# Gate operands made a block product later, in tiles of their own, ordered behind the MLP's casts one per step; the last gate tile multiplied by column halves

## The chip, the cores and the metric

The kernel runs on one core of one Trainium2 chip. The metric is device time in microseconds (us) of one launch. The kernel before took 1662.34 us, the median of three runs (1661.71 to 1663.44).

The engines in the tables: PE is the matmul engine and PEld its weight loads, DVE and ACT are the vector and the scalar engine, POOL is GpSimd, SP the engine that issues most of the DMA transfers. POOL has a DMA queue of its own.

## What is computed

One layer of an encoder with 1024 tokens and 1024 channels: a mixing part (windowed attention beside a bidirectional recurrence), then the two parts that matter here.

```python
hf = rms_norm(x, norm_ffn[i])
x = x + jnp.square(jax.nn.relu(hf @ w_ff1[i])) @ w_ff2[i]      # 1024 -> 4096 -> 1024
hp = rms_norm(x, norm_ple[i])
x = x + (p[i] @ w_ple[i]) * jax.nn.sigmoid(hp @ w_ple_gate[i])  # gate: 1024 x 1024
```

All inputs, weights and the output are float32. The change lies in the second matrix of the MLP (`w_ff2`), during which the operands of the gate matrix (`w_ple_gate`) are prepared, and in the last product of the gate.

## The kernel before, in words

**Split products.** Every float32 product is made of three matmuls on the reduced type fp32r. `split` turns a tile into a high part, a cast on ACT (line 205), and a low part, the tile minus its high part on DVE (line 206). The three terms are high x high, high x low and low x high. In names, an `h` or `l` at the end marks the parts: `sh`, `sl` of a left block and `th`, `tl` of a right block.

**Seven products instead of eight.** The matrices `w_ff2` and `w_ple_gate` are cut into 2 x 2 blocks and multiplied by the Strassen-Winograd scheme: seven block products of sums of blocks. The list `PRODS` gives their order for `w_ff2`: A11 x B11, S2 x T2, A12 x B21, S3 x T3, S1 x T1, A22 x T4, S4 x B22. In the code the loop variable `ip` counts them from 0 to 6; the text calls them product 1 to 7. Their left operands (hidden activations and their sums) lie in DRAM as `hid_...`. The right operands are blocks of `w_ff2` or sums of blocks that `right_of` makes with DVE subtractions. `t1r`, `t2r` and `b11r` are kept in the on-chip memory for a while.

**Steps.** A product has 16 steps (`p` from 0 to 15). A step loads a left block into `sst` and, where needed, a right block into `tst` (three buffers each, issued by SP, 256 KB each), splits both, and issues 12 matmuls of 512 columns on PE (line 2024): four row groups, each into its own PSUM bank, by three terms. `sh`, `sl`, `th` and `tl` have five buffers each (`NR2 = 5`) in the pool `F2`. At the end of product 1 its four banks are copied to `c1r`. At the end of every other product four additions on DVE (`add_to`, line 1881) put the banks into the result `X`. The copy `c1r` has to go into three quarters of `X` besides, in twelve more additions, which are written into the first twelve steps of product 4.

**Gate operands.** `gate_operands` is a generator that prepares the seven right operands of the gate product (T1, B11, T3, T2, B22, T4, B21) for each of four row blocks `k`. A call of it does one operand of one `k`: it makes a sum if one is needed (on DVE, line 1856, in a tile `gsum`), splits the sum or the raw block, and stores the two parts to DRAM (`gop_...`, line 1900) by POOL's queue. It also issues loads of later raw blocks (`graw`, line 1896), again by POOL's queue. The parts are put in the same tiles `th` and `tl` that the MLP's steps use. The call sites lie in products 2 to 5: one at the end of product 2, ten each in products 3 and 5, eight in product 4, and those that are left at the end of product 5 (29 calls, of which the first only loads).

```python
            if ip == 1 and p == NPR - 1 or ip in (2, 4) and p % 5 < 3 or ip == 3 and p % 2:
                next(gops, None)
```

**What sets the order.** The program is written as one sequence; a scheduler orders each engine's instructions from the dependencies and the place in the text, and hands out a tile's buffer again when its last readers are done. `after(ins, prev)` ties one instruction behind another on the same engine, in program order and without a semaphore. A matmul issued by `mmo` (line 232 in the profile) is kept in program order on PE.

**The gate product and the end.** During product 7 the first gate operands are read back from DRAM on SP (`right_gate`, line 1962) and the normed tokens are transposed. After it come the gate's seven products (`product_of`), each of four row tiles `i` of twelve matmuls. `finish` (lines 2113 to 2117) adds a bank to the collected sums, applies the tanh on ACT, multiplies by the stored `p @ w_ple`, adds to `X` and stores the output. The very last tile (A12 x B21, `i == 3`) is finished in two parts of 256 columns.

## Time and profile before

| | |
|---|---|
| median of the runs | 1662.34 us |
| profiled execution | 1661.47 us, span of its trace 1659.7 us |
| PE busy | 1599.7 us, 96% of the span, 12232 matmuls |
| PEld busy | 1291.6 us, 78% |
| DVE busy | 1175.5 us, 71% |
| ACT busy | 872.8 us, 53% |
| POOL busy | 141.3 us, 9% |
| DMA, mean over the span | 185 GB/s |

Busy times are sums over instructions and their share is of the span. Matmuls are pipelined, so their records overlap, and a PE that counts as busy need not run at its peak. Where a row says `[4.16 <-DMA gop_T<-th]`, the engine stood idle for 4.16 us just before the instruction, and the last event that released it was the DMA that stores `th` to `gop_T`. Names are cut at the first digit, so `gop_T` stands for T1, T2, T3 and T4, `gop_B` for B11, B21 and B22, and `hid_S` for S1 to S4. A group's row in the list of waits gives the total time, the number of waits and the longest.

### The profile page before, as it was taken

Reading aid. Unit: us, or ns where it says so; the run is one execution under the profiler, and the core shown is the slowest. Engines: PE = TensorE matmul, PEld = TensorE weight load, DVE = VectorE, ACT = ScalarE, POOL = GpSimd, SP = SyncE. Lnnn points to the kernel's source line nnn. Section 1 sums busy time; section 2 is a strip of 40 time slices with the busy share of each in tenths; the row PEclk is TensorE's granted clock in tenths of the full one; section 3 lists DMA queues with packets and bytes.
Section 4 is the critical chain, followed back from the end, with each engine's and each line's share of the span. In section 5 each row is a group of like instructions: output and inputs, shape, how many; then the busy total and the mean of one; then the engine's idle time right before and its main releaser. Section 6 shows DMA issues by size and latency. Waiting matters only on the chain.

```text
span 1659.7 us, 31568 instructions
## 1 busy us (share of the span) xinstructions
PE 1599.7 (96%) x12232; PEld 1291.6 (78%) x12232; DVE 1175.5 (71%) x2164; ACT 872.8 (53%) x1616; POOL 141.3 (9%) x214
## 2 busy tenths in 40 slices
PE   7999999999999999899999999999999989899998
PEld 7987777666777777677888788888888767788886
DVE  6758998378848769678637866766668767687357
ACT  5558888388554563654324544444444434455452
POOL 1440000300000000000001000000000122200201
PEclk9999999999999999999999999999999999999999
DMA  6363556954575753467721454444489866668456
GB/s 226 83 158 109 165 167 187 271 154 142 166 200 177 210 151 118 159 216 239 262 87 66 140 176 147 139 152 153 153 296 322 250 236 224 205 219 286 156 202 228
DMA packets 212167, 307.02 MB, mean 185 GB/s; under 512 B 49841, under 2 KB 106289, under 8 KB 210737
## 3 DMA queue, kind: packets, MB, share of 16 engines
q1 hardware_dynamic: 192480, 260.43, 48.8%
q0 software_dynamic: 19392, 44.05, 8.6%
q8 instruction: 96, 1.57, 0.4%
q10 hardware_dynamic: 144, 0.52, 0.1%
q14 instruction: 55, 0.44, 0.1%
HBM read 205.33 MB, written 99.61 MB: 184 GB/s over the span
## 4 chain that ended last, share of the span: by engine, by line
PE 66%; DVE 10%; DMA 9%; issue 7%; ACT 6%; POOL 2%; DVEq 0%; SPq 0%; POOLq 0%; ACTq 0%
PE ff1ps L1694 16%; PE ff2ps L2024 8%; PE gps L232 5%; PE gmm L232 4%; DMA wst<-in_w_col_dram 2%; PE mm L250 2%; PE mm L251 2%; PE mm L252 2%; PE psq L468 1%; PE psq L470 1%; PE psq L469 1%; PE mmo L252 1%; PE mmo L250 1%; PE mmo L251 1%; PE wy L232 1%
## 5 line engine op out<-in xcount | busy, mean ns | idle before, releaser
L2024 PE MATMUL ff2ps<-tl,sh 128*128 128x512 f32 x448 | 179.0, 400 | 16.9 <-DVE tl L206 16.9
L2024 PE MATMUL ff2ps<-th,sh 128*128 128x512 f32 x448 | 177.2, 396 | 1.8 <-ACT th L205 1.8
L2024 PE MATMUL ff2ps<-th,sl 128*128 128x512 f32 x448 | 176.7, 394 | 0.0
L2024 PEld LDWEIGHTS ff2ps<-tl,sh 128*128 128x128 f32 x448 | 85.5, 191 | 40.8 <-DVE tl L206 23.3
L205 ACT CAST whi<-wst 128x512 fp32r<-128x512 f32 x100 | 60.1, 618 | 86.4 <-DMA wst<-in_w_col_dram 39.8
L2024 PEld LDWEIGHTS ff2ps<-th,sh 128*128 128x128 f32 x448 | 85.5, 191 | 21.4 <-ACT th L205 3.3
L2024 PEld LDWEIGHTS ff2ps<-th,sl 128*128 128x128 f32 x448 | 85.7, 191 | 17.5
L1694 PE MATMUL ff1ps<-mh,w1h 128*128 128x512 f32 x224 | 87.5, 391 | 0.3 <-ACT w1h L205 0.3
L1694 PE MATMUL ff1ps<-ml,w1h 128*128 128x512 f32 x224 | 87.4, 390 | 0.0
L1694 PE MATMUL ff1ps<-mh,w1l 128*128 128x512 f32 x224 | 87.2, 389 | 0.0
L205 ACT CAST sh<-sst 128x512 fp32r<-128x512 f32 x109 | 67.4, 619 | 37.4 <-DMA sst<-hid_A 13.2
L206 DVE TENSOR_TENSOR sl<-sst,sh 128x512 fp32r<-128x512 f32 x109 | 74.6, 685 | 14.1 <-ACT sh L205 13.8
L205 ACT CAST w1h<-w1st 128x512 fp32r<-128x512 f32 x48 | 28.3, 619 | 98.9 <-DMA w1st<-in_w_ff_dram 64.3
L206 DVE TENSOR_TENSOR wlo<-wst,whi 128x512 fp32r<-128x512 f32 x88 | 58.9, 686 | 17.5 <-ACT whi L205 15.4
L206 DVE TENSOR_TENSOR w1l<-w1st,w1h 128x512 fp32r<-128x512 f32 x48 | 31.8, 687 | 53.4 <-ACT w1h L205 53.4
L1208 DVE TENSOR_TENSOR gm<-gps,gmask 128x384 f32<-128x384 f32 x64 | 32.7, 549 | 30.6 <-PE gps L232 30.4
L238 PE MATMUL gmm<-hh,whi 128*128 128x512 f32 x128 | 51.5, 402 | 1.8 <-ACT whi L205 1.7
L232 PE MATMUL gmm<-hh,wlo 128*128 128x512 f32 x128 | 53.2, 416 | 0.0
L206 DVE TENSOR_TENSOR w1l<-ssum,w1h 128x512 fp32r<-128x512 f32 x64 | 42.8, 685 | 14.3 <-ACT w1h L205 14.3
L232 PE MATMUL gmm<-hl,whi 128*128 128x512 f32 x128 | 52.9, 413 | 0.0
L232 PE MATMUL gmm<-hh,whi 128*128 128x512 f32 x128 | 52.8, 412 | 0.0
L242 PE MATMUL gmm<-hh,wlo 128*128 128x512 f32 x128 | 51.6, 403 | 0.7 <-POOL wlo L206 0.5
(470 smaller groups left out, 4618.9 us busy)
## 6 DMA issues: line engine op xcount, KB each, us to landing
tst<-in_w_ff_dram SPq DMA_DIRECT2D x80, 256.0 KB, 4.2
wst<-in_w_col_dram SPq DMA_DIRECT2D x76, 256.0 KB, 4.1
w1st<-in_w_ff_dram SPq DMA_DIRECT2D x32, 512.0 KB, 4.9
hid_S<-h SPq DMA_DIRECT2D x64, 256.0 KB, 2.1
sst<-hid_S SPq DMA_DIRECT2D x64, 256.0 KB, 4.0
hid_A<-h SPq DMA_DIRECT2D x48, 256.0 KB, 2.0
sst<-hid_A SPq DMA_DIRECT2D x45, 256.0 KB, 4.6
ra_d<-ra SPq DMA_DIRECT2D x8, 1024.0 KB, 5.9
```

The costliest lines, as they stand in the source:

```text
L205: a = nc.scalar.copy(hi, src)
L206: b = (lo_eng or nc.vector).tensor_tensor(out=lo, in0=src, in1=hi.bitcast(F32), op=ALU.subtract)
L232: tc.keep_in_program_order(nc.tensor.matmul(*a, **kw))
L238: mm(ps, ah, bh, start=(i == 0), stop=False)
L242: mm(ps, al, bh, start=False, stop=(i == n - 1))
L250: nc.tensor.matmul(ps, ah, bh, start=(i == 0), stop=False)
L251: nc.tensor.matmul(ps, ah, bl, start=False, stop=False)
L252: nc.tensor.matmul(ps, al, bh, start=False, stop=(i == n - 1))
L468: nc.tensor.matmul(pss[g], ah, wq[k][0][:, gs], start=(k == 0), stop=False)
L1208: a = (nc.vector.tensor_tensor(out=gm[hf][:, s % NB, e].rearrange("p (a b) t -> p a b t", b=2), in0=pss[e][:, 0:6].rearrange("p (a b) t -> ...
L1694: (mmo if p < 2 else nc.tensor.matmul)(ps, x_[:, k, :], y_[:, k, :], start=start and k + i == 0, stop=k == 3 and i == 2, skip_group_check= ...
L2024: nc.tensor.matmul(banks[bs][i], x_[:, isl], y_, start=fresh and p + j == 0, stop=p == NPR - 1 and j == 2, skip_group_check=True)
```

## The change

The diff makes five edits.

1. The parts of gate operands go into tiles `gth` and `gtl` of their own, three buffers each, in the pool `QP`. To make room, `gsum` has one buffer instead of two, T3's sum is written over the raw block B12, `QP` is opened only after product 3 in the place of `c1r`, and `QP` and `t1r` are closed after product 6 instead of product 5. Line numbers in the new program are shifted by 3 to 6 (the closing additions are line 1887, the gate operands' stores line 1906).
2. So that `c1r` is free by then, its twelve additions are written into product 3 instead of product 4.
3. The calls of the generator move: eight in product 4 (its first step and the odd ones from 3 on), fourteen in product 5 (every step from 2 on), the rest in product 6.
4. Each gate step's sum, cast and subtraction are tied by `after` behind the cast or subtraction that the MLP issued last (`paced`), on ACT and on DVE.
5. The last gate tile's twelve matmuls of 512 columns become two sets of twelve of 256 columns, the first half of the columns and then the second, in one bank.

```diff
--- before.py
+++ after.py
@@ -1824,9 +1824,13 @@
         f, n = p + NPR * (int(b[1]) - 1), int(b[2]) - 1
         return w2[f * P:(f + 1) * P, 512 * n:512 * n + 512]
 
-    def parts_of(pl, names, src_, bufs):
+    paced = []
+
+    def parts_of(pl, names, bufs, src_, behind=None):
         hi, lo = (pl.tile([P, 512], F32R, name=x_, bufs=bufs) for x_ in names)
-        split(hi, lo, src_)
+        ops = split(hi, lo, src_, behind=behind)
+        if not behind:
+            paced[:] = ops
         return hi, lo
 
     def fetch(pl, src_, name, bufs):
@@ -1836,8 +1840,8 @@
 
     pre = []
     for p in range(NPRE):
-        pre.append(parts_of(RF, ("sh", "sl"), fetch(RF, hid_d["A11"][p], "st", 1), NPRE)
-                   + parts_of(RF, ("th", "tl"), fetch(RF, w2_block(p, "B11"), "st", 1), NPRE))
+        pre.append(parts_of(RF, ("sh", "sl"), NPRE, fetch(RF, hid_d["A11"][p], "st", 1))
+                   + parts_of(RF, ("th", "tl"), NPRE, fetch(RF, w2_block(p, "B11"), "st", 1)))
     sFO.close()
     sW1.close()
     sM.close()
@@ -1851,9 +1855,11 @@
     def acc(bs, name="ff2ps"):
         return PH.tile([P, 512], F32, name=name, tag=f"acc{bs}", bufs=4)
 
-    def sum_of(op, a_, b_, out_=None):
+    def sum_of(op, a_, b_, out_=None, pace=False):
         o_ = F2.tile([P, 512], F32, name="tmp", bufs=2) if out_ is None else out_
-        nc.vector.tensor_tensor(out=o_, in0=a_, in1=b_, op=op)
+        a = nc.vector.tensor_tensor(out=o_, in0=a_, in1=b_, op=op)
+        if pace:
+            after(a, paced[1])
         return o_
 
     def t1_of(p):
@@ -1896,33 +1902,30 @@
                 nc.gpsimd.dma_start(raw[b], gate_block(k, b))
 
         def keep(k, r, src_):
-            for x_, t_ in enumerate(parts_of(F2, ("th", "tl"), src_, NR2)):
+            for x_, t_ in enumerate(parts_of(QP, ("gth", "gtl"), 3, src_, paced)):
                 nc.gpsimd.dma_start(gop_d[r][x_][:, k, :], t_.bitcast(F32))
-
-        def gsum():
-            return QP.tile([P, 512], F32, name="gsum", tag="gsum", bufs=2)
 
         raw = {}
         for b in ("B11", "B12", "B22"):
             load(0, b)
         yield
         for k in range(4):
-            t = sum_of(ALU.subtract, raw["B12"], raw["B11"], gsum())
+            t = sum_of(ALU.subtract, raw["B12"], raw["B11"], QP.tile([P, 512], F32, name="gsum", bufs=1), True)
             keep(k, "T1", t)
             yield
             keep(k, "B11", raw["B11"])
             load(k, "B21")
             yield
-            keep(k, "T3", sum_of(ALU.subtract, raw["B22"], raw["B12"], gsum()))
+            keep(k, "T3", sum_of(ALU.subtract, raw["B22"], raw["B12"], raw["B12"], True))
             load(k + 1, "B11")
             yield
-            sum_of(ALU.subtract, raw["B22"], t, t)
+            sum_of(ALU.subtract, raw["B22"], t, t, True)
             keep(k, "T2", t)
             yield
             keep(k, "B22", raw["B22"])
             load(k + 1, "B12")
             yield
-            sum_of(ALU.subtract, raw["B21"], t, t)
+            sum_of(ALU.subtract, raw["B21"], t, t, True)
             keep(k, "T4", t)
             yield
             keep(k, "B21", raw["B21"])
@@ -2016,8 +2019,8 @@
             if ip == 0 and p < NPRE:
                 sh, sl, th_, tl_ = pre[p]
             else:
-                sh, sl = parts_of(F2, ("sh", "sl"), fetch(F2, hid_d[lr_][p], "sst", 3), NR2)
-                th_, tl_ = parts_of(F2, ("th", "tl"), right_of(p, rr_), NR2)
+                sh, sl = parts_of(F2, ("sh", "sl"), NR2, fetch(F2, hid_d[lr_][p], "sst", 3))
+                th_, tl_ = parts_of(F2, ("th", "tl"), NR2, right_of(p, rr_))
             for i in range(4):
                 isl = slice(i * P, (i + 1) * P)
                 for j, (x_, y_) in enumerate(((sh, th_), (sh, tl_), (sl, th_))):
@@ -2029,10 +2032,9 @@
                 sX0.close()
                 PXX = pool(sX, "x1", side="right")
                 X = [PXX.tile([P, 4, DM], F32, name=f"X{e}") for e in range(2)]
-                c1 = pool(sC1, "c1", side="right").tile([P, 4, 512], F32, name="c1r")
                 t2r = pool(sT2, "t2", side="right").tile([P, NPR, 512], F32, name="t2r")
                 t1r = pool(sT1, "t1", side="right").tile([P, NPR, 512], F32, name="t1r")
-                QP = pool(sQP, "gprep", side="right")
+                c1 = pool(sC1, "c1", side="right").tile([P, 4, 512], F32, name="c1r")
             if ip == 0 and 0 <= p - (NPR - T1EARLY - NPRE) < NPRE:
                 q = p - (NPR - T1EARLY - NPRE)
                 nc.sync.dma_start(b11[:, q], w2_block(q, "B11"))
@@ -2042,13 +2044,10 @@
                 e, i = divmod(p // 2, 4)
                 t = torder[4 * e + i]
                 nc.sync.dma_start(X[e][:, i, :], x1_d[t * P:(t + 1) * P, :])
-            if ip == 3 and p < 12:
+            if ip == 2 and p < 12:
                 add_to(*((0, 1), (1, 1), (1, 0))[p // 4], p % 4, c1[:, p % 4])
-            if ip == 1 and p == NPR - 1 or ip in (2, 4) and p % 5 < 3 or ip == 3 and p % 2:
+            if ip == 3 and (p == 0 or p > 1 and p % 2) or ip == 4 and p > 1 or ip == 5 and p in (2, 4, 6, 8, 10, 12, 13, 14):
                 next(gops, None)
-            if ip == 4 and p == NPR - 1:
-                for _ in gops:
-                    pass
             if ip == 5 and p % 4 == 1:
                 k, nsl = p // 8, slice(512 * (p // 4 % 2), 512 * (p // 4 % 2) + 512)
                 split(wp[0][:, k, nsl], wp[1][:, k, nsl], fetch(F2, wpv[:, k, nsl], "tst", 3))
@@ -2069,17 +2068,20 @@
             else:
                 for e, n in {1: [(0, 1)], 2: [(0, 0)], 3: [(1, 1)], 4: [(1, 1)], 5: [(1, 0)], 6: [(0, 1)]}[ip]:
                     add_to(e, n, i, b_)
+        if ip == 2:
+            sC1.close()
+            QP = pool(sQP, "gprep", side="right")
         if ip == 3:
             sB11.close()
         if ip == 4:
-            sQP.close()
-            sT1.close()
             PP = pool(sP, "plew")
             wp = [PP.tile([P, 2, DM], F32R, name=f"wp{i}", bufs=1) for i in range(2)]
             pps = []
         if ip == 5:
+            assert next(gops, 0) == 0
+            sQP.close()
+            sT1.close()
             sT2.close()
-            sC1.close()
             RP = pool(sRP, "gate", side="right")
             GL["S1"], GL["A22"] = left(RP, 0), left(RP, 1)
             singles = [slice(k, k + 1) for k in range(4)]
@@ -2095,11 +2097,13 @@
     g12 = LP.tile([P, 4, 512], F32, name="g12", bufs=1)
     cs_ = {n: [LP.tile([P, 512], F32, name=n, tag=f"{n}{i}", bufs=1) for i in range(4)] for n in ("gc5", "gc4", "gc1", "gu2")}
 
-    def product_of(bank, l, r, i, fresh=True):
+    halves = (slice(0, 256), slice(256, 512), slice(0, 512))
+
+    def product_of(bank, l, r, i, fresh=True, cols=slice(0, 512)):
         (lh, ll), (rh, rl) = GL[l], GR[r]
         for k in range(4):
             for j, (x_, y_) in enumerate(((lh, rh), (lh, rl), (ll, rh))):
-                mmo(bank, x_[:, k, tsl(i)], y_[:, k, :], start=fresh and k + j == 0, stop=k == 3 and j == 2, skip_group_check=True)
+                mmo(bank[:, cols], x_[:, k, tsl(i)], y_[:, k, cols], start=fresh and k + j == 0, stop=k == 3 and j == 2, skip_group_check=True)
 
     def finish(e, n, i, name, bank, parts=1):
 
@@ -2161,7 +2165,8 @@
         finish(0, 1, i, "gu2", kept[i])
     for i in R4:
         b_ = acc(0, "gps2")
-        product_of(b_, "A12", "B21", i)
+        for c in halves[:2] if i == 3 else halves[2:]:
+            product_of(b_, "A12", "B21", i, cols=c)
         finish(0, 0, i, "gc1", b_, 2 if i == 3 else 1)
     sF.close()
     sRP.close()
```

**How instructions move.** Three places. The rows give an engine's instructions in the order of its program, with the line, the operation, output and inputs, the shape, and in brackets the semaphores waited for with their engine (`DMAHW` are transfers issued by SP, `DMASW` those issued by POOL).

On DVE, at the start of product 3: the closing additions of product 2 among the first splits of product 3. Before:

```order
L206 TENSOR_TENSOR tl<-tst,th 128x512 [waits DMAHW3_49,Activation_49]
L206 TENSOR_TENSOR tl<-graw,th 128x512 [waits DMASW1_49,Activation_49]
L206 TENSOR_TENSOR sl<-sst,sh 128x512 [waits DMAHW5_49,PE_49,Activation_49]
L1881 TENSOR_TENSOR X_13620<-X_13620,ff2ps 128x512 [waits PE_49] x4
L206 TENSOR_TENSOR tl<-tst,th 128x512 [waits DMAHW4_49,Activation_49]
L206 TENSOR_TENSOR tl<-gsum,th 128x512 [waits DMASW3_49,Activation_49]
L206 TENSOR_TENSOR tl<-tst,th 128x512 [waits DMAHW6_49,Activation_49]
L206 TENSOR_TENSOR sl<-sst,sh 128x512 [waits DMAHW7_49]
```

The change:

```order
L206 TENSOR_TENSOR tl<-tst,th 128x512 [waits DMAHW4_49,Activation_49]
L206 TENSOR_TENSOR sl<-sst,sh 128x512 [waits DMAHW5_49,PE_49,Activation_49]
L1887 TENSOR_TENSOR X_13620<-X_13620,ff2ps 128x512 [waits PE_49] x4
L1887 TENSOR_TENSOR X_13620<-X_13620,c1r 128x512 [waits DVE_49] x3
L206 TENSOR_TENSOR tl<-tst,th 128x512 [waits DMAHW6_49,Activation_49]
L1887 TENSOR_TENSOR X_13620<-X_13620,c1r 128x512 [waits DVE_49]
L206 TENSOR_TENSOR sl<-sst,sh 128x512 [waits DMAHW7_49,Activation_49]
L206 TENSOR_TENSOR tl<-tst,th 128x512 [waits DMAHW0_49,Activation_49]
```

The gate operands' subtractions (`tl<-graw`, `tl<-gsum`) have left this place, and the additions of `c1r` stand behind the closing additions. In both programs the closing additions come only after the low parts of the first three steps of the new product.

On ACT, in product 5: the casts of MLP steps and gate steps. Before:

```order
L205 CAST th<-graw 128x512 [waits DMASW3_49,DMASW2_49,DVE_49]
L205 CAST sh<-sst 128x512 [waits DMAHW7_49,PE_49]
L205 CAST th<-t1r 128x512 [waits PE_49]
L205 CAST th<-gsum 128x512 [waits DMASW5_49,DVE_49]
L205 CAST sh<-sst 128x512 [waits DMAHW2_49,PE_49]
L205 CAST th<-t1r 128x512 [waits PE_49]
L205 CAST th<-graw 128x512 [waits DMASW4_49,DMASW0_49,DVE_49]
L205 CAST sh<-sst 128x512 [waits DMAHW5_49,PE_49]
L205 CAST th<-t1r 128x512 [waits PE_49]
L205 CAST sh<-sst 128x512 [waits DMAHW6_49,PE_49]
L205 CAST th<-t1r 128x512 [waits DMASW2_49,DVE_49]
```

The change:

```order
L205 CAST gth<-gsum 128x512 [waits DMASW6_49,DVE_49,Activation_49]
L205 CAST th<-t1r 128x512 [waits PE_49]
L205 CAST gth<-graw 128x512 [waits DMASW5_49,DMASW1_49,Activation_49]
L205 CAST sh<-sst 128x512 [waits DMAHW2_49,PE_49]
L205 CAST th<-t1r 128x512 [waits PE_49]
L205 CAST gth<-gsum 128x512 [waits DMASW2_49,DVE_49,Activation_49]
L205 CAST sh<-sst 128x512 [waits DMAHW3_49,PE_49]
L205 CAST th<-t1r 128x512 [waits PE_49]
L205 CAST gth<-graw 128x512 [waits DMASW6_49,DMASW0_49,Activation_49]
```

Before, the last cast shown, of the MLP's `th`, waits for a transfer of POOL's queue; in the change the MLP's casts wait for PE alone, and the `gth` casts wait for POOL's transfers, one such cast behind each MLP step.

On DVE, at the end of the program, in the change (before it reads the same but for the line numbers):

```order
L2117 TENSOR_TENSOR gc_16962<-gc_16962,gps_17576 128x256 [waits PE_49]
L2117 TENSOR_TENSOR gc_16962<-gc_16962,gps_17576 128x256
L2119 SCALAR_TENSOR_TENSOR gc_16962<-gc_16962,pwl 128x256 [waits DMASW3_49,Activation_49]
L2119 SCALAR_TENSOR_TENSOR gc_16962<-gc_16962,pwl 128x256 [waits Activation_49]
L2120 TENSOR_TENSOR X_13620<-X_13620,gc_16962 128x256 [waits DVE_49] x2
```

The two additions of 256 columns that read the last bank stand side by side, and only the first of them carries a wait for PE.

## The prediction

> **What bounds the kernel now.** I read the product stage from coarse to fine. First the windows, cut at every 192nd matmul of line 2024, so that each row is one of the first six products of the second MLP matrix. A product is sixteen steps of twelve matmuls. Columns: length, then per engine busy time and instructions (PE, PEld, DVE, ACT, POOL), granted clock, DMA share, GB/s.
>
> ```profile
> span 1659.7 us, 31568 instructions
> ...
> 1212.34:1256.87 44.53, 44.26 (x194) 35.88 (x192) 34.90 (x55) 20.63 (x34) 0.55 (x1) 1.00 0.96 344
> 1256.87:1300.39 43.52, 43.52 (x194) 36.04 (x192) 37.76 (x61) 19.93 (x35) 1.09 (x2) 1.00 0.89 292
> 1300.39:1356.86 56.47, 48.06 (x193) 36.68 (x192) 31.93 (x52) 21.32 (x39) 12.43 (x23) 0.97 0.78 255
> 1356.86:1407.44 50.58, 46.07 (x193) 36.94 (x192) 40.19 (x67) 24.57 (x45) 10.81 (x20) 0.97 0.62 204
> 1407.44:1460.53 53.09, 47.51 (x194) 37.75 (x192) 32.80 (x54) 23.54 (x43) 12.43 (x23) 0.94 0.64 211
> 1460.53:1504.05 43.52, 43.52 (x194) 36.05 (x192) 33.75 (x55) 19.81 (x36) 0.00 (x0) 1.00 0.74 236
> ```
>
> Products 2 and 6 take 43.52 us and PE is never idle in them: the floor is 2.72 us a step. Products 3, 4 and 5 lie above it by 12.95, 7.06 and 9.57 us, 29.58 us together, and POOL, which issues the gate operands' transfers, is busy in just these three. Product 1 loses 1.01 us. No engine is full where the time is lost: DVE has 31.93 us of work in the 56.47 of product 3. So the loss is waiting, not work. The waits inside the same stretch, 1212 to 1504 (total us, times, longest):
>
> ```profile
> ACT th L205 <- DMA gop_T<-th: 25.4, 9, 4.4
> ...
> ACT th L205 <- DMA gop_B<-th: 22.9, 7, 4.7
> ...
> DVE tl L206 <- DMA gop_T<-tl: 18.2, 9, 3.6
> ...
> DVE tl L206 <- DMA gop_B<-tl: 17.3, 9, 4.5
> PE ff2ps L2024 <- DVE tl L206: 16.9, 15, 3.4
> ...
> PE ff2ps L2024 <- ACT th L205: 1.8, 3, 0.7
> ```
>
> ACT waits 48.3 us and DVE 35.5 us for the stores of gate operands, because MLP steps and gate steps draw th and tl from the same five buffers, and a buffer that held a gate operand is free only when its store has landed. PE then waits 18.7 us for tl and th. The first stall of product 3, in the timelines of ACT, POOL, DVE and PE (start, length):
>
> ```profile
> 1297.20 0.62 ACT L205 CAST th<-gsum 128x512 fp32r<-128x512 f32 x1
> ...
> 1303.64 0.62 ACT L205 CAST th<-graw 128x512 fp32r<-128x512 f32 x1 [4.16 <-DMA gop_T<-th]
> ```
>
> ```profile
> 1298.12 0.54 POOL L1900 DMA_DIRECT2D gop_T<-th  x1 [75.73 <-ACT th L205]
> ```
>
> ```profile
> 1304.29 0.69 DVE L206 TENSOR_TENSOR tl<-graw,th 128x512 fp32r<-128x512 f32 x1 [3.74 <-ACT th L205]
> 1304.90 0.69 DVE L206 TENSOR_TENSOR sl<-sst,sh 128x512 fp32r<-128x512 f32 x1
> 1305.51 2.47 DVE L1881 TENSOR_TENSOR X<-X,ff2ps 128x512 f32<-128x512 f32 x4
> 1307.90 0.69 DVE L206 TENSOR_TENSOR tl<-tst,th 128x512 fp32r<-128x512 f32 x1
> ```
>
> ```profile
> 1305.83 0.39 PE L2024 MATMUL ff2ps<-th,sh 128*128 128x512 f32 x1
> 1308.64 0.80 PE L2024 MATMUL ff2ps<-tl,sh 128*128 128x512 f32 x1 [2.42 <-DVE tl L206]
> 1309.23 0.63 PE L2024 MATMUL ff2ps<-th,sl 128*128 128x512 f32 x1
> 1309.66 0.63 PE L2024 MATMUL ff2ps<-th,sh 128*128 128x512 f32 x1
> ...
> 1312.15 0.39 PE L2024 MATMUL ff2ps<-th,sh 128*128 128x512 f32 x1
> ```
>
> One gate cast takes a buffer at 1297.20, its store is issued at 1298.12, and the next gate cast, which draws the same buffer, starts only at 1303.64, with the MLP's casts queued behind it on ACT and DVE. PE stands from 1305.83 to 1308.64. After that its matmuls start 0.43 us apart (1309.23, 1309.66), not 2.72/12 = 0.227, and the eight intervals up to 1312.15 take 3.51 us instead of 1.82: a long stall is paid again in a lower granted clock, 0.94 to 0.97 in these windows against 1.00. That is why 29.58 us are lost where the named idle time is 18.7.
>
> **The change part by part.** *Own buffers for gate operands.* gth and gtl, three each, so the MLP's five th and tl are freed by PE alone. No cast or store is added. The 83.8 us of ACT and DVE waiting on buffers that the MLP shares go. What remains is the gate operands' own set, reused after three gate steps: 8.16 us at one step per MLP step (product 5), 16.3 at one per two (products 4 and 6). What has to fit in:
>
> ```profile
> L1900 POOL DMA_DIRECT2D gop_T<-tl x16: 539/539/547, 1298.9 to 1451.5; - x16
> ...
> DMA to landing us min/median/max: 2.7/4.7/7.6
> ```
>
> The store's median 4.7 us, two POOL issues of 0.54 and a DVE subtraction of 0.69 make 6.5 us, less than 8.16. The longest, 7.6, makes 9.4, over by 1.2 us once. Queued behind such a wait stand the next MLP casts, and PE waits only when their lead is gone. On DVE the four additions that close a product, which must wait for its last matmul, stand behind the tl of the third step of the next product, so the lead there is about three steps, 8.2 us; elsewhere the five buffers allow more.
>
> *Steps moved and tied.* The 28 gate steps and their loads run in products 4 to 6 (7, 14, 7) and each stands behind the MLP casts of its step. The twelve c1 additions move into product 3 or before. DVE starts such instructions 0.60 us apart:
>
> ```profile
> 1384.04 0.68 DVE L206 TENSOR_TENSOR sl<-sst,sh 128x512 fp32r<-128x512 f32 x1
> 1384.64 0.68 DVE L206 TENSOR_TENSOR tl<-gsum,th 128x512 fp32r<-128x512 f32 x1
> ```
>
> Counted from the code, DVE then has per product: third, 32 splits + 4 closing additions + at most 12 of c1 = 48, 28.8 us; fourth, 48 + 4 + 7 gate splits + 4 gate sums = 63, 37.8; fifth, 32 + 4 + 14 + 8 = 58, 34.8; sixth, 48 + 4 + 7 + 4 + 4 of w_ple = 67, 40.2. All are under 43.52. The sixth is the tightest: it carried 55 and now has 3.3 us to spare. A sum directly followed by its split holds DVE for one ACT cast, 0.62 us; a few of these use up the spare but not the lead. On ACT a gate cast is one more 0.6 us beside two per step of 2.72. Cover gone, each microsecond that DVE lacks in the sixth product is one on PE.
>
> *Transfers.* The transfers here are of 256 KB:
>
> ```profile
> sst<-hid_S SPq DMA_DIRECT2D x64, 256.0 KB, 4.0
> ...
> gop_T<-tl POOLq DMA_DIRECT2D x16, 256.0 KB, 4.4
> ```
>
> A gate step issues two stores and, four times in seven, a load. In product 5 that is 2.57 + 1 MLP load = 3.57 transfers, 936 KB in 2.72 us, 344 GB/s, where the third to fifth products moved 204 to 255. The row nearest is product 1: 344 GB/s on average, and in its middle more, with PE full:
>
> ```profile
> 1234.00:1254.00 20.00, 20.00 (x90) 16.57 (x89) 18.85 (x30) 10.99 (x19) 0.00 (x0) 1.00 1.03 380
> ```
>
> Product 6 needs about two MLP loads a step, half a gate step and four w_ple loads: some 325 GB/s. I charge products 5 and 6 what product 1 lost at this load, 1.01 us each, together 2.0. The lower bound is 0 (product 2 lost nothing at 292); the upper one is the rival below. On SP, the gate loads for the last stage wait for these stores. Before, there was room, last store to first load:
>
> ```profile
> 1456.84 0.54 POOL L1900 DMA_DIRECT2D gop_B<-tl  x1 [1.38 <-DVE tl L206]
> ```
>
> ```profile
> 1493.34 0.38 SPq L1962 DMA_DIRECT2D grh<-gop_T  x1
> ```
>
> Now the last store follows step 13 of product 6, about when the loads begin (33 us into the product). But the loads go by T1 first, whose last block is stored at step 2, and the last T4 load stands some thirty SP rows behind the first, so I charge nothing.
>
> *Last gate tile by halves.* Twelve matmuls of 512 columns become 24 of 256. Spacings there are, for 512 and 384 columns:
>
> ```profile
> 1653.14 0.39 PE L232 MATMUL gps<-grl,glg 128*128 128x512 f32 x1
> 1653.37 0.39 PE L232 MATMUL gps<-grh,glgs 128*128 128x512 f32 x1
> ```
>
> ```profile
> 25.02 0.33 PE L470 MATMUL psq<-wqh,hl 128*128 128x384 f32 x1
> 25.19 0.33 PE L468 MATMUL psq<-wqh,hh 128*128 128x384 f32 x1
> ```
>
> 0.227 and 0.174 us; on the line through them 256 columns give 0.121, so 24 x 0.121 = 2.90 against 2.72, +0.2 us. If they cost as much as 384 columns, 4.2, +1.5. The gain would be that the first half's additions start early. But in the new program only the first of the two additions carries a wait for PE and the second none, so that one wait covers all 24 matmuls and both start together as before. If it did not, at most the first half's 1.45 us would be gained. I take +0.2.
>
> **A rule beside the rows.** The Trainium skill, TensorE: Matmul & The Clock Gate, section "What's actually happening", lets the array fall to half rate only after about 3.4 us idle. This trace disagrees in part: half spacing followed a record of 2.42 us idle. By the rule a leftover stall of 2 to 3 us would cost only itself; by the row it costs some 1.7 us more (3.51 less 1.82). The 2.0 us charged above come in small pieces, so the sum is the same by both.
>
> **The sum.** The profiled execution took 1661.47 us (span 1659.7, 1.8 around it). 1661.47 - 12.95 - 7.06 - 9.57 + 2.0 + 0.2 = 1634.1 us. It lies 0.9 under the median of the runs before, 1662.34, which is within their spread; I forecast **1634 us**, 1.7% faster.
>
> **The rivals.** *A, chance 0.70:* the sum above, 1630 to 1638.
>
> *B, 0.17: the gate operands' own set becomes the wait.* For: product 5 issues fourteen steps in a row, and the stretches that mixed these stores with loads moved no more than 255 GB/s. At that rate a step of 936 KB takes 3.67 us instead of 2.72, 14 x 0.95 = 13.3 us, of which the lead hides 8.2; some 5 us stay, with a slow clock behind them and as much again in the dense end of product 6: about 1643. Against: 255 GB/s was measured while the queues themselves stood waiting, and 380 was moved for 20 us. The skill's DMA: Bandwidth & Descriptors, section "Where 436 GB/s comes from", puts a core's memory limit at about 358 GB/s, which would leave product 5 almost no reserve; the row of 380 is above it, so I give it no more weight.
>
> *C, 0.06: the gate operands come too late.* They are finished some 20 us nearer to their use; if SP stands at a gate load for one landing, up to 7.6 us, product 7's loads queue behind it: 1634 + 8 = 1642.
>
> *D, 0.03: the shared buffers were not the cause*, and the MLP's casts stay late for another reason (the four closing additions, the loads): 1660, no change.
>
> *E, 0.04, the other side: the ties make every gate wait an MLP wait.* On both ACT and DVE the next MLP cast stands behind the gate cast. If a store under the new load lands after L us, a gate step costs (L + 1.8)/3; over fourteen steps, less 8.2 of lead, this eats 29.6 us when it exceeds 2.72 by 2.7, so from L = 14.5 on the kernel is slower; at 16 it is 14 x 3.2 - 8.2 - 29.6 = +7, 1668. Against it: the longest landing in the trace is about half of that.
>
> Faster by over 0.2% (3.3 us, about what a measurement of this kernel can tell from no change): A, B and C, 0.93. Same: 0.03. Slower: 0.04. The range goes from a full recovery with product 1's 1.01 us and an early first half (1630) to B with a bad product 6 (1645).
>
> **What would show it.** Right: all of products 1 to 6 within 2 us of 43.52 in the windows; no wait of th or tl on a gop store; waits of gth and gtl on gop stores without PE idle behind them; 330 to 350 GB/s in product 5; the last two 256-column additions back to back after the last matmul, as before. Wrong: idle PE in products 5 and 6 behind DVE tl, with gtl waiting for gop (B, E); idle PE after 1504 of the old time behind sst loads (C); PE idle in product 3, where no gate step is left (D).

## The result

The changed kernel took 1637.36 us, the median of six runs (1634.04 to 1639.73), against 1661.03 for six runs of the kernel before (1658.39 to 1663.44). The ratio is 0.9855, 95% interval 0.9838 to 0.9872: 1.45% faster, some 24 us. The forecast was 1634 with a range of 1630 to 1645, so time and sign were as predicted. The way there was not: one loss of 8 us was missed, and most of this study is about it.

The profiled execution of the change took 1639.40 us (span 1637.6), one of the longer of the six. Its windows, cut as in the prediction: the first six products, then the stretch from product 7's first matmul to the first gate matmul, then the rest. Columns: length, busy time and instructions of PE, PEld, DVE, ACT and POOL, granted clock, DMA share, GB/s.

```profile
1212.80:1256.42 43.62, 43.62 (x193) 36.04 (x192) 33.91 (x54) 21.23 (x35) 0.00 (x0) 1.00 0.99 350
1256.42:1299.94 43.52, 43.52 (x193) 36.04 (x192) 35.82 (x57) 18.83 (x34) 0.00 (x0) 1.00 0.87 288
1299.94:1343.46 43.52, 43.52 (x193) 36.04 (x192) 30.71 (x50) 20.26 (x35) 0.00 (x0) 1.00 0.62 200
1343.46:1386.98 43.52, 43.52 (x194) 36.04 (x192) 39.07 (x65) 24.31 (x44) 10.95 (x21) 1.00 0.78 240
1386.98:1430.50 43.52, 43.52 (x194) 36.04 (x192) 35.59 (x58) 23.30 (x42) 18.19 (x34) 1.00 0.93 311
1430.50:1475.34 44.84, 44.28 (x194) 35.88 (x192) 34.40 (x56) 20.98 (x39) 8.11 (x15) 1.00 0.84 267
1475.34:1551.44 76.10, 72.00 (x321) 58.35 (x320) 40.86 (x67) 39.93 (x75) 11.33 (x20) 0.98 0.62 209
1551.44:1637.60 86.16, 80.40 (x381) 66.96 (x379) 53.44 (x85) 34.57 (x62) 11.29 (x21) 0.98 0.63 222
```

The last two windows of the kernel before:

```profile
1504.05:1573.51 69.46, 69.19 (x322) 57.39 (x320) 39.42 (x65) 38.06 (x72) 11.33 (x20) 1.00 0.60 203
1573.51:1659.70 86.19, 80.25 (x369) 66.19 (x367) 53.46 (x85) 34.57 (x62) 11.29 (x21) 0.98 0.62 221
```

Products 2 to 5 take 43.52 us each, the floor to the hundredth. Products 3, 4 and 5 gave back 12.95 + 7.06 + 9.57 = 29.58 us and product 1, this time, 0.91. Against that stand 1.32 in product 6, 6.64 in the stretch after it (76.10 against 69.46) and 0.46 ahead of product 1. The end is as long as before, 86.16 against 86.19. The sum, -29.58 - 0.91 + 1.32 + 6.64 + 0.46 - 0.03 = -22.1, is the difference of the two spans.

The waits of the changed kernel in products 1 to 6, where the kernel before had 83.8 us behind the stores of gate operands (total, times, longest):

```profile
ACT wp L205 <- DMA tst<-in_w_ple_dram: 9.3, 3, 4.7
...
DVE gtl L206 <- DMA gop_T<-gtl: 3.6, 2, 3.3
...
PE ff2ps L2027 <- DVE tl L206: 0.6, 2, 0.4
```

The MLP's th and tl wait for no store any more, and the gate operands' own set waits for one twice. From issue to landing the 56 stores of gate operands (line 1906) took, min/median/max:

```profile
DMA to landing us min/median/max: 2.7/4.8/7.0
```

That is later than before: the same 56 stores of the kernel before, by their line 1900, took 2.6/3.7/5.5. (The 2.7/4.7/7.6 of the prediction is a row in which the later loads that read `gop_T` back are counted with its stores.)

What dominates is at the top. The casts of `w_ple` blocks on ACT wait 9.3 us for their loads. The code loads the four blocks in product 6, into the same three `tst` buffers as the MLP's right blocks; one cast runs ahead, in product 4, and three stand in product 6. But this wait is not new. The same window of the kernel before:

```profile
ACT wp L205 <- DMA tst<-in_w_ple_dram: 9.6, 3, 5.0
```

It is as long, and product 6 stood at its floor all the same. The changed kernel pays for a wait that was free before. Around the longest one, on ACT, DVE and PE:

```profile
1456.14 0.62 ACT L205 CAST th<-tmp 128x512 fp32r<-128x512 f32 x1
1461.46 0.62 ACT L205 CAST wp<-tst 128x512 fp32r<-128x512 f32 x1 [4.70 <-DMA tst<-in_w_ple_dram]
1461.98 0.61 ACT L205 CAST sh<-sst 128x512 fp32r<-128x512 f32 x1
1462.50 0.62 ACT L205 CAST th<-tmp 128x512 fp32r<-128x512 f32 x1
```

```profile
1462.11 0.69 DVE L206 TENSOR_TENSOR wp<-tst,wp 128x512 fp32r<-128x512 f32 x1 [1.23 <-ACT wp L205]
1462.72 0.68 DVE L206 TENSOR_TENSOR sl<-sst,sh 128x512 fp32r<-128x512 f32 x1
1463.32 0.68 DVE L206 TENSOR_TENSOR tl<-tmp,th 128x512 fp32r<-128x512 f32 x1
```

```profile
1464.06 0.50 PE L2027 MATMUL ff2ps<-tl,sh 128*128 128x512 f32 x1 [0.39 <-DVE tl L206]
```

ACT stands from 1456.8 to 1461.5 with the MLP's next casts behind the w_ple cast, and DVE's splits follow at once. PE has caught up: the lead of the splits is almost zero as product 7 begins, at 1475.34. Its first low part has only just been made:

```profile
1474.50 0.68 DVE L206 TENSOR_TENSOR tl<-tst,th 128x512 fp32r<-128x512 f32 x1
```

In the kernel before, the same low part was made 6.4 us ahead of product 7, which began at 1504.05:

```profile
1496.98 0.68 DVE L206 TENSOR_TENSOR tl<-tst,th 128x512 fp32r<-128x512 f32 x1
```

Product 7 then carries norms, transposes and the `w_ple` products besides, and its waits reach PE, which before stood 0.27 us in this whole stretch: three waits for low parts, together 1.9 us, and two more. The dearest:

```profile
1514.30 0.50 PE L250 MATMUL pwps<-wp,pp 128*128 128x512 f32 x1 [1.46 <-ACT pwt L2009]
1514.64 0.40 PE L251 MATMUL pwps<-wp,pp 128*128 128x512 f32 x1
...
1515.54 0.63 PE L251 MATMUL pwps<-wp,pp 128*128 128x512 f32 x1
1515.96 0.63 PE L252 MATMUL pwps<-wp,pp 128*128 128x512 f32 x1
```

The matmuls behind it go 0.42 us apart for some 3 us: here, too, a stall is paid a second time in the spacing (granted clock 0.98 in this stretch, 1.00 before).

### The profile page after: what moved, and what is told of

The parts are those of the page before. It is cut to its first block, busy times and chain, and to the rows that moved or that the text cites. A ratio compares the mean times of both kernels' runs of the same rounds, so it can differ in the third digit from the quotient of the medians.

```text
span 1637.6 us, 31595 instructions
## 1 busy us (share of the span) xinstructions
PE 1588.2 (97%) x12244; PEld 1286.9 (79%) x12244; DVE 1175.0 (72%) x2164; ACT 873.8 (53%) x1616; POOL 140.4 (9%) x214
## 4 chain that ended last, share of the span: by engine, by line
PE 69%; DVE 11%; ACT 8%; DMA 7%; issue 4%; POOL 1%; SPq 0%; DVEq 0%; ACTq 0%; POOLq 0%
PE ff1ps L1694 16%; PE ff2ps L2027 13%; PE gps L232 5%; PE gmm L232 4%; DMA wst<-in_w_col_dram 2%; PE mm L250 2%; PE mm L251 2%; PE mm L252 2%; PE mmo L251 1%; PE mmo L250 1%; PE mmo L252 1%; PE wy L232 1%; PE psq L468 1%; PE psq L469 1%; PE psq L470 1%
## 5 line engine op out<-in xcount | busy, mean ns | idle before, releaser
L2027 PE MATMUL ff2ps<-tl,sh 128*128 128x512 f32 x448 | 175.0, 391 | 2.5 <-DVE tl L206 2.5
```

Source lines behind the costliest of these rows:

```text
L2027: nc.tensor.matmul(banks[bs][i], x_[:, isl], y_, start=fresh and p + j == 0, stop=p == NPR - 1 and j == 2, skip_group_check=True)
```

## The experiments

Eleven kernels, in three sets; those of a set ran on one chip beside the kernel before. Since the work ahead of this part begins product 1 anywhere from 1208.0 to 1214.5 us in these profiles, the single steps are read from the lengths of the windows, and the total from the runs. "The stretch" is that from product 7's first matmul to the first gate matmul.

| kernel | median us | ratio to before, 95% interval |
|---|---|---|
| before, stores read the source | 1645.31 | 0.9913, 0.9891 to 0.9935 |
| change, th and tl shared again | 1663.89 | 1.0021, 1.0001 to 1.0041 |
| change, gate steps earlier | 1633.84 | 0.9844, 0.9817 to 0.9871 |
| change, without ties | 1637.26 | 0.9866, 0.9841 to 0.9891 |
| change, again | 1636.69 | 0.9865, 0.9842 to 0.9889 |
| change, w_ple in a buffer of its own | 1629.77 | 0.9816, 0.9795 to 0.9838 |
| change, two gth and gtl | 1641.82 | 0.9889, 0.9873 to 0.9905 |
| change, three edits together | 1631.14 | 0.9822, 0.9805 to 0.9839 |
| before, w_ple in a buffer of its own | 1661.44 | 1.0002, 0.9987 to 1.0017 |
| change, no ties, w_ple in its own buffer | 1637.46 | 0.9847, 0.9823 to 0.9871 |
| change, last tile in whole rows | 1638.55, one run | - |

### Are the stores in the shared buffers the cause? From before

```diff
-            for x_, t_ in enumerate(parts_of(F2, ("th", "tl"), src_, NR2)):
-                nc.gpsimd.dma_start(gop_d[r][x_][:, k, :], t_.bitcast(F32))
+            parts_of(F2, ("th", "tl"), src_, NR2)
+            for x_ in range(2):
+                nc.gpsimd.dma_start(gop_d[r][x_][:, k, :], src_)
```

> The kernel before, with one edit: a gate operand's two stores read the raw block or the sum it was made from, not th and tl (so the stored operands are not split and the output differs from the reference). All gate steps, casts, subtractions, stores and loads stay at their old places; a buffer of th or tl is held by no store any more. Theory 1 (the shared ring, held by stores, was the cause): the waits of th and tl on gop stores vanish (they were 48.3 us on ACT and 35.5 on DVE), products 3 to 5 come down from 56.47, 50.58 and 53.09 us to within 3 us of 43.52 each, the total falls by 20 to 30 us, to about 1631-1640. Rival (the gate steps' own work at these places was the cause, or the late closing additions): products 3 to 5 stay above 48 us and the total above 1650. A part of the gain may be eaten by sums that now wait for the stores on DVE.

Measured: 1645.31 us, 15 below before, between what the two theories said. No wait of th or tl on a store is left. Windows of products 1, 3, 4 and 5:

```profile
1210.69:1259.03 48.34, 45.78 (x194) 35.65 (x193) 32.24 (x51) 19.25 (x32) 4.81 (x9) 1.00 0.98 345
...
1306.13:1353.53 47.40, 45.44 (x193) 37.10 (x192) 34.99 (x57) 23.20 (x42) 12.37 (x23) 0.96 0.84 276
1353.53:1397.74 44.21, 44.19 (x193) 35.70 (x192) 38.56 (x64) 22.51 (x42) 9.67 (x18) 1.00 0.74 251
1397.74:1445.67 47.93, 44.55 (x193) 35.99 (x193) 38.52 (x63) 26.91 (x50) 9.12 (x17) 1.00 0.66 218
```

Products 3 to 5 lost 8.98 us in place of 29.58. So at least 20.6 us hung on stores that hold th and tl. The 9 that are left stand behind sums that now wait for raw blocks (`gsum` behind a load of `graw`, 4.76 us once, with a PE stall of 1.96 behind it). These waits came to 8.9 us, against 1.9 before, and the edit itself can have made them, since a raw block is now held until its stores have landed; that was not separated. Products 1 and 2 lost 8.4 us. In product 1 a likely cause is the edit too: without a split to wait for, stores went out as soon as a raw block was there (nine POOL issues in product 1, where before there was one), on top of this product's dense loads. The loss in product 2 was not traced. The theory holds for most of the loss, and the edit was not clean.

### The same question from the other side

```diff
-            for x_, t_ in enumerate(parts_of(QP, ("gth", "gtl"), 3, src_, paced)):
+            for x_, t_ in enumerate(parts_of(F2, ("th", "tl"), NR2, src_, paced)):
```

> The changed kernel with one part undone: the parts of gate operands go back into the MLP's th and tl (five buffers shared), while the steps stay where the change put them, tied one behind each MLP step, and c1's additions stay in product 3. Theory 1: the waits on gop stores are back in products 4 to 6, PE stalls behind th and tl, worst in product 5 with its fourteen steps; product 3 stays at 43.5; the total is 1652 to 1670. Rival (moving and tying alone did it): products 4 to 6 stay within 3 us of 43.52 and the total is below 1642.

Measured: 1663.89 us, 0.2% slower than before. Products 4, 5 and 6, and the waits of this part:

```profile
1347.41:1394.00 46.59, 44.41 (x194) 35.81 (x192) 32.97 (x55) 20.46 (x37) 9.28 (x18) 1.00 0.56 175
1394.00:1455.77 61.77, 51.91 (x193) 38.84 (x192) 37.39 (x61) 26.63 (x48) 19.90 (x37) 0.92 0.76 243
1455.77:1510.37 54.60, 47.87 (x193) 36.50 (x192) 42.35 (x69) 24.79 (x45) 8.09 (x15) 0.97 0.81 266
```

```profile
ACT th L205 <- DMA gop_T<-th: 24.3, 12, 3.3
DVE tl L206 <- DMA gop_T<-tl: 24.3, 10, 4.0
```

The loss is where the steps are: 3.1, 18.3 and 11.1 us in products 4 to 6. With shared tiles, moving and tying are worth nothing; the whole gain hangs on the tiles of their own.

### Are the gate steps in product 6 to blame for its loss?

```diff
-            if ip == 3 and (p == 0 or p > 1 and p % 2) or ip == 4 and p > 1 or ip == 5 and p in (2, 4, 6, 8, 10, 12, 13, 14):
+            if ip == 3 and (p == 0 or p > 1 and p not in (4, 7, 10)) or ip == 4 or ip == 5 and p in (0, 1):
```

> The changed kernel with the gate steps taken out of product 6: twelve in product 4, sixteen in product 5, one in product 6's first step. Theory H1 (product 7 and the step ahead of it lost 6.6 + 1.3 us because seven gate steps in product 6 use up the lead of ACT and DVE that product 7 needs): product 6 is back at 43.5, the stretch from product 7's first matmul to the first gate matmul falls from 76.1 to 69-71 us, total 1629 to 1633, if product 4 (DVE about 42 us of work by count) stays within 1 us of its floor. Rival H2 (product 7's loss comes from its own loads, transposes and norms, whatever product 6 holds): the stretch stays at 75 or more and the total at 1636 or above. Rival H3: the loss only moves, into product 4, which then exceeds 45 us.

Measured: 1633.84 us. Product 6 and the stretch:

```profile
1429.14:1475.00 45.86, 43.85 (x194) 35.97 (x192) 32.80 (x54) 19.09 (x35) 0.00 (x0) 1.00 0.75 239
1475.00:1543.90 68.90, 68.90 (x321) 57.38 (x320) 39.45 (x65) 38.12 (x72) 11.33 (x20) 1.00 0.61 206
```

The stretch fell from 76.10 to 68.90, as H1 said, and products 4 and 5 stayed at 43.52, with eleven and sixteen steps (the first of the twelve calls in product 4 only loads). But product 6, now with one gate step, lost more, 2.34 us. One stall holds all of it, on ACT and PE:

```profile
1434.69 0.62 ACT L205 CAST wp<-tst 128x512 fp32r<-128x512 f32 x1 [5.80 <-DMA tst<-in_w_ple_dram]
```

```profile
1439.69 0.50 PE L2027 MATMUL ff2ps<-tl,sh 128*128 128x512 f32 x1 [2.00 <-DVE tl L206]
```

That was in no expectation. It pointed to the `w_ple` load as a cause of its own, the rival H4 below.

### What are the ties worth?

`behind=paced` and the tie of the sums were taken out; the steps' own tiles and their places in the text stayed.

> The changed kernel without the ties: sums, casts and subtractions of gate steps are not tied behind the MLP's. By the written order of ACT and DVE the scheduler then puts gate casts several steps ahead, beginning in product 3, and often two or three in a row ahead of one MLP step. Theory T1 (with own buffers the ring of three still binds; bunched gate casts wait for stores with the MLP's casts behind them, and the ties are what spreads them): waits of gth and gtl on gop stores of over 20 us, PE stalls of 5 to 20 us in products 3 to 5, total 1642 to 1658. Rival T2 (own buffers alone do it, the ties are worth nothing): total within 3 us of 1637.

Measured: 1637.26 us, the same as the change. The windows of products 3 and 4:

```profile
1297.85:1343.98 46.13, 44.78 (x194) 35.72 (x192) 36.35 (x60) 24.10 (x43) 17.63 (x33) 1.00 0.90 323
1343.98:1393.38 49.40, 46.30 (x194) 36.91 (x193) 46.48 (x78) 28.57 (x52) 17.55 (x34) 0.97 0.89 307
```

The scheduler put the steps ahead into products 3 and 4, which lost 2.6 and 5.9 us; products 5, 6 and the stretch lost nothing (43.52, 43.52, 68.90). ACT's order shows the wait, two gate casts in a row ahead of an MLP step:

```profile
1321.44 0.62 ACT L205 CAST gth<-gsum 128x512 fp32r<-128x512 f32 x1 [2.12 <-DMA gop_T<-gth]
1325.50 0.62 ACT L205 CAST gth<-graw 128x512 fp32r<-128x512 f32 x1 [3.44 <-DMA gop_T<-gth]
```

T2's time came out, but not its reason: the ties do remove 8.5 us of stalls, and about as much was lost at the other end, by the `w_ple` load. Waits of gth and gtl on stores came to 18.6 us, where over 20 were expected.

### The change again, and the rival H4

> The changed kernel itself, unaltered, beside the other three on one chip, since executions of it lay between 1634.0 and 1639.7 us. Expected 1637 us, products 1 to 5 together within 5 us of 217.6 us (5 x 43.52), product 6 at 44 to 46, the stretch from product 7's first matmul to the first gate matmul at 72 to 76 us; if that stretch varies between executions while products 3 to 5 do not, the spread of this kernel's times comes from it.

```diff
-            if ip == 5 and p % 4 == 1:
+            if ip == 5:
                 k, nsl = p // 8, slice(512 * (p // 4 % 2), 512 * (p // 4 % 2) + 512)
-                split(wp[0][:, k, nsl], wp[1][:, k, nsl], fetch(F2, wpv[:, k, nsl], "tst", 3))
+                if p % 4 == 0:
+                    wst = fetch(PP, wpv[:, k, nsl], "wplst", 1)
+                if p % 4 == 3:
+                    split(wp[0][:, k, nsl], wp[1][:, k, nsl], wst, behind=paced)
```

> The changed kernel, with the four loads of w_ple in product 6 into a staging tile of their own, issued three steps ahead of their cast, instead of a tst buffer shared with the MLP's right blocks; gate steps stay where the change put them. Theory H1 (seven gate steps in product 6 use up the lead): product 6 and the stretch after it stay as in the changed kernel (44.8 and 72 to 76 us), total within 2 us of 1637. Rival H4 (the lead is lost where ACT stands at the cast of a w_ple block, 3.33 and 4.70 us in the trace, with the MLP's casts behind it): product 6 at 43.5 to 44, the stretch at 69-70, total 1629 to 1633.

Measured: 1636.69 us for the change (1633.13 to 1639.85) and 1629.77 with the `w_ple` edit (1626.81 to 1632.37), on one chip. Product 6 and the stretch of the first:

```profile
1427.37:1471.31 43.94, 43.87 (x194) 35.92 (x192) 33.89 (x56) 20.91 (x38) 8.13 (x15) 1.00 0.83 274
1471.31:1545.16 73.85, 70.47 (x321) 57.19 (x321) 41.51 (x69) 39.97 (x75) 11.37 (x20) 1.00 0.65 216
```

And of the second, with the gate steps of product 6 in their place:

```profile
1431.50:1475.02 43.52, 43.52 (x193) 36.04 (x192) 36.12 (x60) 22.80 (x42) 7.58 (x14) 1.00 0.96 325
1475.02:1543.93 68.91, 68.91 (x322) 57.36 (x320) 38.47 (x64) 37.41 (x71) 11.37 (x20) 1.00 0.59 201
```

H4 holds: products 2 to 6 are at the floor to the hundredth, the stretch is at 68.91, and no `w_ple` cast waits. It does so at 325 GB/s in product 6, so the transfers themselves were no limit there. Product 7's first low part is made 8 us ahead of that product (1466.28 against 1475.02). H1 alone falls: seven gate steps cost product 6 nothing once the `w_ple` loads stand aside. The edit does four things at once (a buffer of its own, a load three steps ahead, a cast two steps later in the text, a tie), and which of them is needed was not separated.

The second profile of the unaltered change also shows where two executions of it differ. Its span is 6.2 us shorter: 3.13 of it ahead of product 1, 0.90 in product 6, 2.25 in the stretch; products 2 to 5 agree to the hundredth. (Product 6, at 43.94, came out just below the 44 to 46 expected.) The 2.25 are 0.72 of idle time, as the stall of 0.73 us is missing, and 1.53 of busy time: here the wait of 1.47 us for `pwt` was followed by matmuls 0.23 us apart.

### Is the w_ple load a loss by itself? And do both repairs add up?

The same edit in the kernel before, and in the change without ties:

> The kernel before, with only the w_ple edit: its four loads into a staging tile of their own, three steps ahead of their cast, the cast tied behind the MLP's. Theory (the w_ple cast costs something only where gate steps in product 6 have already used the slack; in the kernel before there are none, product 6 ran at 43.52 and the stretch after it at 69.46): no change, 1657 to 1662. Rival (the w_ple loads on the tst ring are a loss of their own): 1651 to 1655, as in the changed kernel, where this edit gave 6.9 us.

> The changed kernel without the ties and with the w_ple edit. Without ties the scheduler puts the gate steps ahead, products 3 and 4 lost 2.6 and 5.9 us and product 6 and the stretch after it nothing. Theory (the ties move the bunched steps out of products 3 and 4, and what they leave is the w_ple wait in product 6; so each repair is needed, and only both give 1630): total 1635 to 1639, products 3 and 4 together 6 us or more above 87.04, stretch 68.9. Rival (the ties are not needed once the w_ple loads are off the tst ring): total 1629 to 1632.

Measured: 1661.44 and 1637.46 us, no change in either, ratio 1.0002 (0.9987 to 1.0017) in the first. In the kernel before, products 3 to 5 stay at 56.35, 50.76 and 55.10 us and product 6 at 43.52; without ties, products 3 and 4 stay at 45.95 and 49.53. So in these kernels the late `w_ple` load costs something only where gate steps lie close by, in product 5's last and product 6's steps, and have used up what hid it. With gate steps bunched early (no ties) or before (no steps in product 6), the same edit is worth nothing. Of the kernels tried with gate steps at these places, only the one with both ties and `w_ple` edit reaches 1629.77.

### How near to its limit is the set of three?

`gth` and `gtl` with two buffers each instead of three.

> The changed kernel with two gth and gtl each instead of three. This prices the gate operands' own set. By the prediction's formula a gate step then costs (4.7 + 1.8)/2 = 3.25 us in product 5 where the step has 2.72: 14 x 0.53 = 7.4 us, of which a lead of 8.2 hides nearly all in product 5, and the debt is paid in product 6 and 7: total 1637 to 1645, with waits of gth and gtl on gop stores of 10 us or more. Rival (stores land soon enough, the set is not near its limit): within 2 us of the changed kernel.

Measured: 1641.82 us, some 5 over the change. Product 5 and 6:

```profile
1384.71:1428.23 43.52, 43.52 (x193) 36.04 (x192) 33.43 (x54) 22.15 (x40) 18.42 (x34) 1.00 0.88 287
1428.23:1476.33 48.10, 44.69 (x193) 35.81 (x192) 36.91 (x60) 22.22 (x41) 8.13 (x15) 1.00 0.85 271
```

The waits on gop stores before gth and gtl come to 8.2 us, all in product 5: near the formula's 7.4, below the 10 expected. Product 5 hides them in its lead, and the debt falls due in product 6, where PE stands 1.98 and 1.44 us, each time just after a `w_ple` cast that waited (3.14 and 5.18 us). So the 5 us are the price of two buffers beside the late `w_ple` load; two buffers with the `w_ple` edit were not tried. (Products 1 and 2 of this profile, ahead of any gate step, lost 2.6 us besides.) Three buffers were enough.

### The last tile's halves

```diff
-        for c in halves[:2] if i == 3 else halves[2:]:
+        for c in halves[2:]:
```

> The changed kernel with the last gate tile multiplied in whole rows of 512 columns again. Prediction's term: 24 x 0.121 in place of 12 x 0.227 costs 0.2 us, so the stretch from the first gate matmul to the end should be 86.0 instead of 86.16. Rival read from the trace (DVE still finishes the third tile when the last matmul ends, so PE's 0.2 us is hidden): 86.2, no difference.

Measured: the last stretch is 86.19 us, against 86.16 and 86.24 in the two profiles of the change: no difference. The end of the changed kernel on PE and DVE:

```profile
1631.44 0.28 PE L232 MATMUL gps<-grl,glg 128*128 128x256 f32 x1
1631.56 0.28 PE L232 MATMUL gps<-grh,glgs 128*128 128x256 f32 x1
```

```profile
1631.65 0.69 DVE L2120 TENSOR_TENSOR X<-X,gc 128x512 f32<-128x512 f32 x1
1632.26 0.74 DVE L2117 TENSOR_TENSOR gc<-gc,gps 128x256 f32<-128x256 f32 x2
```

The matmuls of 256 columns are 0.12 us apart, as estimated. The last one ends at 1631.84, but DVE is still at the third tile and comes to the last additions at 1632.26. PE's 0.2 us is hidden behind DVE.

### Three edits together

The early gate steps, the `w_ple` edit, and the halves in two PSUM banks, so that the first half's addition waits for its own twelve matmuls.

> Three edits to the changed kernel: the gate steps as in the run with twelve in product 4, sixteen in product 5 and one in product 6; the four loads of w_ple into a staging tile of their own, three steps ahead of their cast; the last gate tile's halves in two PSUM banks, so that the first half's addition waits for its twelve matmuls alone. Theory: products 2 to 6 all at 43.5, the stretch after them at 68.9, and the time from the last matmul to the end falls from 6.0 us by 0.4 to 0.8; total 1627 to 1632. Rival: the 2.3 us that product 6 lost in the run with early gate steps stays (it came from the closing additions or the sixteen steps in a row, not from the w_ple load), total 1632 to 1635.

Measured: 1631.14 us, no better than the `w_ple` edit alone (the intervals overlap). Products 2 to 6 are at 43.52, the stretch at 68.91, so the rival falls: with the `w_ple` loads aside, the closing additions and the sixteen steps in a row cost product 6 nothing. The first half's addition now runs at 1619.41, ahead of the last matmul at 1620.53, in a gap in which DVE waited for ACT:

```profile
1619.41 0.42 DVE L2120 TENSOR_TENSOR gc<-gc,gps 128x256 f32<-128x256 f32 x1 [0.21 <-PE gps L232]
...
1621.79 0.42 DVE L2120 TENSOR_TENSOR gc<-gc,gps 128x256 f32<-128x256 f32 x1
```

The last stretch takes 85.99 us, 0.2 less than otherwise: below the 0.4 to 0.8 expected, and below what the runs can tell.

## Why the prediction was right, and where it was wrong

**What bounds the kernel: right.** The 29.58 us above the floor came back whole, in both profiles of the change. One run took away the stores' hold on th and tl, and at least 20.6 us with it, another put it back; both moved products 3 to 6 as the reading of the waits said. Rival D (the shared buffers are not the cause) is out.

**Own set of three, rivals B and E: right to set them low.** Stores landed in 2.7 to 7.0 us, and product 5 moved 311 GB/s, less than the 344 estimated. Two buffers gave nearly the waits that the formula gives, so the formula fits and three lie on its safe side. Its landing term was right by luck: 4.7 us came from a row that counts read-backs with the stores, the stores alone had a median of 3.7, and in the change it rose to 4.8. E needed 14.5 us of landing.

**The residual of 2.0 us: mis-sized in place and size.** It charged 1.01 each to products 5 and 6, after product 1's loss at the same GB/s. Product 5 lost nothing, product 6 1.32 (0.42 in the second profile). Load in GB/s was the wrong measure: with the `w_ple` edit product 6 moved 325 GB/s at its floor.

**The step that failed: "a few of these use up the spare but not the lead".** The count of DVE's work was near enough: 229 instructions in the windows of products 3 to 6 against 236 counted (in the sixth 56 against 67, since splits run ahead of PE and part of them falls into the product before). But the step asked only whether the work fits. It did not ask what else on ACT waits for a landing there. The `w_ple` cast waited 9.6 us in the kernel before, where nothing was lost by it, and the prediction passed over that row. The change put gate casts around it, the lead went to almost zero, and the next stretch, which has waits of its own, lost 6.64 us (4.39 in the second profile). The sum had no term for that stretch.

**Rival C: wrong in its mechanism.** It gave 8 us in about the place where 8 were lost, but through SP standing at gate loads until late stores have landed, and in SP's list of waits no gate load waits for a store. The sign set for C did appear: ACT's first casts of product 7 wait for sst loads (4.11, 0.88 and 3.13 us), and PE idles behind low parts that follow. But the run with the `w_ple` edit leaves the gate stores and gate loads where they were in the text, has two such waits too (3.06 and 2.99 us), and PE loses nothing: what the change lacks is the lead that covers them.

**The halves: right that nothing is gained, wrong on why.** One wait covers all 24 matmuls, as the order shows, but that is not what binds: DVE is late anyway, which also hides the 0.2 us charged.

So 1661.47 - 29.58 gives 1631.9; the forecast added 2.2 for the rest, and the profile 7.5. The median, 1637.36, still lies in A's 1630 to 1638, and that is partly luck: the loss that no term named was small beside what came back, product 1 gave back 0.91 that was not forecast, and the profiled execution, at 1639.40, lies outside A.

## What to carry to other kernels

A buffer that two streams share is freed at the pace of the slower reader: if one of them goes out by DMA, give it a ring of its own, and size the ring by (landing + issue + split) over the time between steps. When work is moved into a stage that looks half empty, list the waits that the stage already has, also those that cost nothing, since the lead that hides them is what the moved work consumes. And look one stage further: a debt of lead falls due where the next dense stage begins.

## What the runs showed of the hardware

- Whether the half-rate spacing of 0.43 us follows a stall does not go by the stall's length alone. It followed PE stalls of 1.96 us (stores read from the source), 1.79 (no ties) and 1.46 with 0.73 shortly ahead (the change); it did not follow 2.00 (early gate steps) and 2.04 (stores read from the source). Even the same wait for `pwt` differs: 1.47 us was followed by half rate in the run with two gth and gtl, by full rate in the second profile of the change. What decides was not tried.
- The core moved 350 GB/s on average over product 1's 43.62 us (the change), and 325 in product 6 at its floor of 43.52 (the run with the `w_ple` edit), with no idle time of PE in either.
